# Pacing the transfers that sum weights, and handing over the activations of the down projection one by one

## The chip, the cores and the metric

The kernel runs on one core of a Trainium2 chip. The metric is the device time of one execution in microseconds (us): here the median of three runs of the kernel before, and later of the runs of the changed kernel beside it.

## The reference, cut to what matters

Two transformer-like blocks run one after the other on a sequence of 1024 tokens with 1024 features, all in float32. What the change touches lies at three places: the modulation vectors at the very start, the up projection, and the down projection.

```python
def modulation(c, w, b, n):
    m = jax.nn.silu(c) @ w + b
    return jnp.split(m, n, axis=-1)

def modulated_norm(x, g, shift, scale):
    return rmsnorm(x, g) * (1.0 + scale[:, None, :]) + shift[:, None, :]

def short_conv_layer(x, c, mod_w, mod_b, norm_g, w_in, conv_w, w_out):
    shift, scale, gate = modulation(c, mod_w, mod_b, 3)
    h = modulated_norm(x, norm_g, shift, scale)
    proj = h @ w_in
...
def _conv_ffn(h, w_up, conv_w, conv_b, w_down):
    u = h @ w_up
    a, g = jnp.split(u, 2, axis=-1)
    s = a.shape[1]
    ap = jnp.pad(a, ((0, 0), (CONV_WIDTH - 1, 0), (0, 0)))
    a = ap[:, 0:s] * conv_w[0] + ap[:, 1:s + 1] * conv_w[1] + ap[:, 2:s + 2] * conv_w[2] + conv_b
    return (jax.nn.gelu(a, approximate=False) * g) @ w_down
```

## The kernel before, in words

Activations are kept transposed, features on the partitions and tokens along the free side, in two halves of 512 tokens. Each float32 product is made of three float32r products: a weight tile (a *piece*, `wr`, 128 x 512 elements, 256 KB) is loaded by SP, its rounded part `wh` is written by ScalarE (a CAST), and the rest `wl` by VectorE (a subtraction). Activations are split in the same way into the two halves of an `act` tile. `proj` (line 432) then runs three matmuls for each 128 x 128 block of weights and 512 tokens. Pieces form one list, `stream`, in the order of use; loads run 5 pieces ahead of the use, the casts 3 and the subtractions 2.

The program is written by Python code that keeps a rough clock for each engine (`Sched`). Side jobs are generators: what each one yields says when it wants its next turn on that clock, and `proj` gives turns between its matmuls. So the numbers in `yield` set where in the order an instruction stands, and nothing else: on the chip an engine runs its queue in that order, and waits only for the semaphores of real dependences.

**The start.** SP loads four tiles of x (`xk`, 512 KB each), then strips of the modulation weights (`mw`, two DMAs of 256 KB a strip) with a piece of `w_in` after most of them. VectorE multiplies each strip by silu(c) and adds it up (`acc`); PE sums over partitions (`sm`); VectorE makes `mod_a` and `gs_a` and from these the normed activations `nt`, which ScalarE and VectorE split into `act`. Only then can the first projection (`pj`) run. Four strips give the first quarter of the features.

**The weight sums.** The up projection is done with sums of blocks of its weights, so that fewer products are needed. `weight_sums` (line 1431) has these sums made by 128 DMAs on POOL's queue, from DRAM to DRAM, 64 rows of 1408 elements each (352 KB), some of which add to what stands at their destination. They are first needed in `up_rest`, some 2000 us into the run. POOL's queue also carries the kernel's stores (`x_d`, `k_d`, `v_d`, `q_d`, ...), each of which waits for the engine that makes its data. A POOL DMA waits for no more than the eighth DMA before it on that queue, and for its data.

**The down projection.** It runs over 22 `act` tiles, eight jobs of 66 matmuls for the first half of the tokens, and then eight jobs for each quarter of the second half. The tiles come from DRAM (`act_d`): `act_side` (line 1614) loads one (`al`) and splits it once there is room. Room is a count: `big` tiles in use may not exceed 34, and `free` lowers the count. A half's 22 tiles are given up together by `drop` when the last job (j == 7) is written; the same `drop` serves the other three projections that use `res_jobs` (line 765).

Of the kernel before, what the change touches and what calls it, by code (L numbers as in the profile page):

```python
# [9 lines left out]
F32 = mybir.dt.float32  # L10
# [8 lines left out]
HT = 512  # L19
NJ = 8  # L20
DFF = 2816
NF = DFF // 128
# [26 lines left out]
N_G = 7  # L49
M_BR = 4  # L50
M_WO = 5
T_SUM = 110.0
E_SUM = 9.0
R_SUM = 64


class Sched:
# [204 lines left out]
def tile_body(  # L262
# [14 lines left out]
    sch = Sched()  # L277
# [4 lines left out]
    act = sca.activation  # L282

    const = ctx.enter_context(tc.tile_pool(name="const", bufs=1))
# [9 lines left out]
    out = out[0]  # L294
# [10 lines left out]
    def free(n=1):  # L305

        in_use[0] -= n

    def room(n, hold=0):

        while in_use[0] + n > N4:
            yield 0.4
        in_use[0] += hold
# [5 lines left out]
    def sml(w=HT, dt=F32, name="s"):  # L319
        return s2.tile([128, w], dt, nm(name))  # L320
# [7 lines left out]
    def f32(ap):  # L328
        return ap.bitcast(F32)
# [24 lines left out]
    stream = []  # L354
# [44 lines left out]
    A = {}  # L399

    def split_to(key, src, sh=None):

        yield from room(1 + (kept[0] if key[0] in ("h2", "act0") else 0))
        t = big([2, HT], F32R, "act")
        hi, lo = t[:, 0, :], t[:, 1, :]
        if sh is None:
            sca.copy(out=hi, in_=src)
            if src.space == bass.MemoryType.PSUM:
                sch.keep(src)
            yield t  # L410
            vec.tensor_tensor(out=lo, in0=src, in1=f32(hi), op=ALU.subtract)
        else:
            act(out=hi, in_=src, func=ACTF.Identity, bias=sh)
            yield t
            vec.scalar_tensor_tensor(out=lo, in0=src, scalar=sh, in1=f32(hi), op0=ALU.add, op1=ALU.subtract)
        A[key] = t

    def drop(name, half=None):
        for k in [k for k in A if k[0] == name and (half is None or k[2] == half)]:
            del A[k]  # L420
            free()
# [7 lines left out]

        return half if isinstance(half, tuple) else (half, 0, HT)  # L430

    def proj(pieces, name, half):

        h, c0, w = span(half)
        c = slice(c0, c0 + w)
        sch.turn(sch.bank_time())
        ps = bank("pj")[:, 0:w]
        nk = sum(p.nk for p in pieces)
        k = 0
        for pc in pieces:  # L440
            use(pc)
            for i in range(pc.nk):
                a = act_of((name, k, h))
                sch.turn(sch.when((a, pc.h, pc.l)))
                mm(ps, lhsT=pc.h[:, i, :], rhs=a[:, 0, c], start=k == 0, stop=False)
                mm(ps, lhsT=pc.h[:, i, :], rhs=a[:, 1, c], start=False, stop=False)
                mm(ps, lhsT=pc.l[:, i, :], rhs=a[:, 0, c], start=False, stop=k == nk - 1)
                k += 1
        return ps

# [239 lines left out]
    def hs(half):  # L690
        h, c0, w = span(half)
        return slice(h * HT + c0, h * HT + c0 + w)
# [65 lines left out]
    def res_jobs(w, name, gate, x_dram, out_dram, done=None, extra_g=None, ks=((0, 4), (4, 4)), squares=True, pairs=False):  # L758
        st = {}

        def post(j, half, ps, xo):
            n = span(half)[2]
            if pairs:
                if j % 2 == 0:
                    st["pair", half] = big([2, HT], name="xn")
                xn = st["pair", half][:, j % 2, :]
            else:
                xn = sml(n, name="xn")
            vec.scalar_tensor_tensor(out=xn, in0=ps, scalar=V[gate][:, j:j + 1], in1=xo,
                                     op0=ALU.mult, op1=ALU.add)  # L770
            if out_dram is not None:
                store(out_dram[j, :, hs(half)], xn)
            if done is None:
                return
            s = st.setdefault(half, {"x": [], "acc": [None, None]})
            s["x"].append(xn)
            if squares:
                for a, g in enumerate([None, extra_g]):
                    if a and g is None:
                        continue  # L780
                    yield xn
                    sq = sml(name="sq")
                    act(out=sq, in_=xn, func=ACTF.Square, scale=V[g][:, j:j + 1] if g else 1.0)
                    yield sq
                    if j == 0:
                        s["acc"][a] = sq
                    else:
                        vec.tensor_tensor(out=s["acc"][a], in0=s["acc"][a], in1=sq, op=ALU.add)
                if j == 7:
                    yield s["acc"][0]  # L790
                    yield from done(half, st.pop(half))
            elif j in TURNS:
                yield xn
                yield from done(half, s, j)

        def job(j):
            def fn(half, pieces):
                h, c0, n = span(half)
                xo = sml(n, name="xo")
                syn.dma_start(out=xo, in_=x_dram[j, :, hs(half)])  # L800
                ps = proj(pieces, name, half)
                if j == 7 and c0 + n == HT:
                    drop(name, h)
                then(post(j, half, ps, xo))
            return [Piece(w, k, n, j * 128, 128) for k, n in ks], fn
        return [job(j) for j in range(NJ)]
# [104 lines left out]
    def wait(name):  # L911
        while name not in flags:
            yield 0.5
# [517 lines left out]
    def weight_sums():  # L1431

        def W(k, f, n):
            return w_up[512 * k:512 * k + 512, n * DFF + f * HF:n * DFF + (f + 1) * HF]

        while sch.t < T_SUM:
            yield 2.0
        for n in range(2):
            g = [sg_d[i][n] for i in range(4)]
            for to, of, op in ((0, W(0, 1, n), None), (2, W(0, 0, n), None), (0, W(1, 1, n), ALU.add),  # L1440
                               (2, W(0, 1, n), ALU.add), (1, W(0, 0, n), None), (3, W(1, 0, n), None),
                               (1, g[0], ALU.add), (3, g[1], ALU.add)):
                for r in range(0, 512, R_SUM):
                    kw = {"accum_op": op, "max_dma_last_dim": HF * 4} if op else {}
                    pol.dma_start(out=g[to][r:r + R_SUM], in_=of[r:r + R_SUM], **kw)
                    yield E_SUM

# [166 lines left out]
    def act_side(half):  # L1614

        fs = [f + i for f, n in DOWN for i in range(n)]
        for k, f in enumerate(fs):
            yield from wait(("act", f, half))
            yield from room(1)
            sch.spawn(act_one(k, f, half))  # L1620
            yield 0.7

    def act_one(k, f, half):
        t = sml(name="al")
        syn.dma_start(out=t, in_=act_d[f, :, hs(half)])
        yield t
        yield from split_to(("act", k, half), t)

    fin = {}

# [402 lines left out]
```

## Time and profile before

| | |
|---|---|
| median of 3 runs | 2667.33 us (2665.23 to 2668.66) |
| the profiled execution, its own time | 2669.03 us |
| its span, first to last instruction | 2666.9 us |
| mean granted TensorE clock | 0.992 of full |
| PE busy | 2570.2 us (96%) |
| VectorE, ScalarE, POOL busy | 1724.5, 1232.9, 276.0 us |
| DMA queue of SP (q1), of POOL (q0), of ScalarE (q10), share of 16 engines | 48.6%, 16.2%, 0.4% |

PE is the engine that is nearly always busy, so the time is PE's work, the stretches in which PE stands idle, and the stretches in which it runs at the lower of its two clock levels (2.4 and 1.2 GHz). The spans of an execution and its time differ by some 2 us, which lie around the first and last instruction.

### The profile page before, as it was taken

What the parts mean: (1) busy time and instruction counts of PE and PEld (TensorE: products, weight loads), DVE (VectorE), ACT (ScalarE), POOL (GpSimd) and SP (SyncE); (2) the same over time, 40 slices, a digit from 0 to 9 for tenths busy, and PEclk for the clock granted to TensorE, in tenths of its full rate; (3) what the DMA queues carried; (4) which work ended last, traced back from release to release, by engine and by line L of the source; (5) the groups of instructions that cost most, each with busy time, mean ns of one, the idle gap of its engine ahead of it and who ended that gap; (6) DMA issues with size and microseconds to landing.
All of it is one profiled execution on the core that took longest, in us unless ns stands there. A gap on an engine that the chain in (4) does not pass through costs nothing.

```text
span 2666.9 us, 39606 instructions
## 1 busy us (share of the span) xinstructions
PE 2570.2 (96%) x14015; PEld 2126.0 (80%) x14015; DVE 1724.5 (65%) x3137; ACT 1232.9 (46%) x2492; POOL 276.0 (10%) x469
## 2 busy tenths in 40 slices
PE   2999999999999989999999999999999999999898
PEld 1888888889977767778787887888787788888798
DVE  2876666776366687988765556674657766663454
ACT  2521112353155566777674353564536534443343
POOL 3000000122221111211210110000001000000000
PEclk9999999999999999999999999999999999999999
DMA  9865556778798876666885757555454546454575
GB/s 288 279 190 159 160 170 213 247 240 266 210 252 229 250 194 160 185 200 171 224 222 149 223 159 225 167 158 167 155 164 151 173 138 186 141 170 153 165 212 156
DMA packets 536078, 514.64 MB, mean 193 GB/s; under 512 B 30078, under 2 KB 429704, under 8 KB 535880
## 3 DMA queue, kind: packets, MB, share of 16 engines
q1 hardware_dynamic: 497252, 377.01, 48.6%
q0 software_dynamic: 36272, 130.88, 16.2%
q10 hardware_dynamic: 2356, 4.21, 0.4%
q8 instruction: 111, 1.82, 0.3%
q14 instruction: 87, 0.71, 0.1%
HBM read 422.07 MB, written 136.05 MB: 209 GB/s over the span
## 4 chain that ended last, share of the span: by engine, by line
PE 89%; DVE 5%; DMA 2%; SPq 2%; ACT 2%; issue 1%; DVEq 0%; ACTq 0%
PE pj L246 71%; PE pv L246 5%; PE o L246 4%; PE z L246 4%; PE tr L247 3%; SPq L247 2%; DVE om L247 2%; DVE be L247 1%; DVE wl L247 1%; PE sm L247 1%; DVE act L247 0%; DMA wr<-in_w_in_dram 0%; DMA wr<-in_b_w_out_dram 0%; DMA wr<-in_b_w_qz_dram 0%; DMA wr<-in_a_w_in_dram 0%
## 5 line engine op out<-in xcount | busy, mean ns | idle before, releaser
L246 PE MATMUL pj<-act,wh 128*128 128x512 f32 (+1 forms) x6064 | 1837.5, 386 | 21.1 <-ACT act L247 11.6
L246 PEld LDWEIGHTS pj<-act,wh 128*128 128x128 f32 x6064 | 1099.0, 189 | 239.2 <-ACT act L247 13.1
L246 PE MATMUL pj<-act,wl 128*128 128x512 f32 (+1 forms) x3032 | 1158.6, 382 | 1.4 <-DVE wl L247 1.4
L246 PEld LDWEIGHTS pj<-act,wl 128*128 128x128 f32 x3032 | 572.5, 189 | 122.3 <-DVE wl L247 2.7
L247 DVE TENSOR_TENSOR wl<-wr,wh 128x512 fp32r<-128x512 f32 (+1 forms) x752 | 493.5, 676 | 145.4 <-ACT wh L247 144.1
L247 ACT CAST wh<-wr 128x512 fp32r<-128x512 f32 (+1 forms) x752 | 444.3, 615 | 197.6 <-PE pj L246 81.7
L247 ACT COPY aT<-tr 128x512 f32<-128x512 f32 (+3 forms) x272 | 128.6, 504 | 153.4 <-PE tr L247 149.4
L246 PE MATMUL z<-kd,qs 128*128 128x512 f32 (+2 forms) x704 | 166.3, 352 | 0.0
L247 DVE SCALAR_TENSOR_TENSOR acc<-mw,silu_c,acc 128x512 f32<-128x512 f32 x196 | 146.5, 748 | 30.3 <-DMA mw<-in_a_mod_w_dram 27.0
L246 PE MATMUL pv<-wh,act 128*128 128x256 f32 x768 | 141.0, 282 | 0.0
L247 DVE SCALAR_TENSOR_TENSOR xn<-pj,mod,xo 128x512 f32<-128x512 f32 (+1 forms) x40 | 25.7, 643 | 158.6 <-PE pj L246 158.6
L246 PEld LDWEIGHTS z<-kd,qs 128*128 128x128 f32 x704 | 115.1, 192 | 15.5 <-issue 5.3
L247 DVE TENSOR_TENSOR_SCAN om<-om 128x640 f32<-128x640 f32 (+3 forms) x64 | 120.6, 1884 | 7.6 <-ACT om L247 7.6
L246 PEld LDWEIGHTS pv<-wh,act 128*128 128x128 f32 x768 | 119.3, 188 | 0.1
L246 PEld LDWEIGHTS o<-aT,vp 128*64 128x64 f32 (+1 forms) x1440 | 99.6, 150 | 21.7 <-issue 13.0
L246 PE MATMUL o<-aT,vp 128*64 128x128 f32 (+1 forms) x1440 | 116.1, 281 | 0.7 <-ACT aT L247 0.7
L246 PE MATMUL pv<-wl,act 128*128 128x256 f32 x384 | 107.9, 281 | 0.0
L247 POOL DMA_DIRECT2D x_d<-xn x48 | 26.4, 550 | 653.8 <-DVE xn L247 653.6
L247 ACT ACTIVATE p<-p,t 128x256 f32<-128x256 f32 (+7 forms) x128 | 81.2, 636 | 25.0 <-DVE t L247 24.9
L247 ACT ACTIVATE sq<-xn 128x512 f32<-128x512 f32 x48 | 30.5, 636 | 110.2 <-DVE xn L247 105.1
L247 DVE TENSOR_REDUCE t<-sm 128x4 f32<-128x512 f32 x40 | 27.6, 690 | 81.1 <-PE sm L247 81.1
L247 ACT COPY u<-pj 128x512 f32<-128x512 f32 x38 | 22.3, 587 | 124.4 <-PE pj L246 71.1
(225 smaller groups left out, 2450.7 us busy)
## 6 DMA issues: line engine op xcount, KB each, us to landing
wr<-in_w_in_dram SPq DMA_DIRECT2D x136, 256.0 KB, 3.8
mw<-in_w_ada_dram SPq DMA_DIRECT2D x96, 256.0 KB, 3.7
wr<-in_w_down_dram SPq DMA_DIRECT2D x96, 256.0 KB, 3.1
wr<-in_a_w_in_dram SPq DMA_DIRECT2D x80, 256.0 KB, 6.1
wr<-in_w_up_dram SPq DMA_DIRECT2D x66, 256.0 KB, 3.2
wr<-in_b_w_qz_dram SPq DMA_DIRECT2D x64, 256.0 KB, 5.7
qs<-q_d SPq DMA_DIRECT2D x64, 256.0 KB, 9.0
mw<-in_a_mod_w_dram SPq DMA_DIRECT2D x48, 256.0 KB, 6.2
```

The source lines that it names most:

```text
L246: return f(out, *value, **kw)
L247: return f(out=out, **kw)
```

## The change

Three edits. A POOL instruction, a copy of one column of the `wl` piece that was split last at that place of the program, now stands ahead of each of the 128 summing DMAs, so that POOL reaches the DMA only when VectorE has made that piece; the numbers that place the sums are changed, and on the program's clock none is placed between 600 and 880. `proj` gets a flag with which the last job gives up each `act` tile when its three matmuls are written, in place of the `drop` at the end. And `act_side` loads tiles 5 ahead without asking for room, and asks for it only when it splits one.

```diff
-T_SUM = 110.0
-E_SUM = 9.0
+T_SUM = 130.0
+E_SUM = 6.0
+BUSY_SUM = (600.0, 880.0)
 R_SUM = 64
+AHEAD_ACT = 5
...
-    def proj(pieces, name, half):
+    def proj(pieces, name, half, last=False):
...
                 mm(ps, lhsT=pc.l[:, i, :], rhs=a[:, 0, c], start=False, stop=k == nk - 1)
+                if last:
+                    del A[name, k, h]
+                    free()
                 k += 1
...
-                ps = proj(pieces, name, half)
-                if j == 7 and c0 + n == HT:
-                    drop(name, h)
+                ps = proj(pieces, name, half, j == 7 and c0 + n == HT)
...
+        paced = const.tile([128, 1], F32, name="paced")
         while sch.t < T_SUM:
             yield 2.0
...
                     kw = {"accum_op": op, "max_dma_last_dim": HF * 4} if op else {}
+                    while BUSY_SUM[0] < sch.t < BUSY_SUM[1]:
+                        yield 2.0
+                    pol.tensor_copy(out=paced, in_=f32(stream[done_to["l"] - 1].l[:, 0, 0:1]))
                     pol.dma_start(out=g[to][r:r + R_SUM], in_=of[r:r + R_SUM], **kw)
                     yield E_SUM
...
         fs = [f + i for f, n in DOWN for i in range(n)]
-        for k, f in enumerate(fs):
-            yield from wait(("act", f, half))
-            yield from room(1)
-            sch.spawn(act_one(k, f, half))
-            yield 0.7
-
-    def act_one(k, f, half):
-        t = sml(name="al")
-        syn.dma_start(out=t, in_=act_d[f, :, hs(half)])
-        yield t
-        yield from split_to(("act", k, half), t)
+        got = {}
+        for k in range(NF + AHEAD_ACT):
+            if k < NF:
+                yield from wait(("act", fs[k], half))
+                got[k] = sml(name="al")
+                syn.dma_start(out=got[k], in_=act_d[fs[k], :, hs(half)])
+            if k >= AHEAD_ACT:
+                t = got.pop(k - AHEAD_ACT)
+                yield t
+                yield from room(1)
+                sch.spawn(split_to(("act", k - AHEAD_ACT, half), t))
+            yield 0.6
```

The change moves instructions on all engines, since the clock on which the program is written comes out otherwise. SP's queue is the same row for row up to its 101st DMA, which covers the whole start. The first place is POOL's queue at the start, before (`sg_d0a` and the like are the summing DMAs):

```order
L247 DMA rows_293<-in_final_norm_g_dram 8x128
L247 DMA sg_d0a<-in_w_up_dram 64x1408 x8
L247 DMA sg_d2a<-in_w_up_dram 64x1408 x8
L247 DMA sg_d0a<-in_w_up_dram 64x1408 x8
L247 DMA sg_d2a<-in_w_up_dram 64x1408 x5
L247 DMA x_d<-xn_3606 128x512
```

and the same place of the changed kernel:

```order
L249 DMA rows_293<-in_final_norm_g_dram 8x128
L249 COPY paced<-wl_1439 128x1
L249 DMA sg_d0a<-in_w_up_dram 64x1408
L249 COPY paced<-wl_1439 128x1
L249 DMA sg_d0a<-in_w_up_dram 64x1408
L249 COPY paced<-wl_1522 128x1
L249 DMA sg_d0a<-in_w_up_dram 64x1408
```

Before, 29 sums stood with nothing to wait for ahead of the first store; now each waits for a `wl` that is made after the start, and 39 of them stand ahead of that store. POOL's queue as a whole has these sums, before and now: up to the first store of x 29 and 39; from there to the last store of v 27 and 35; from there to the last store of q 21 and none; from there to the end of the first half of `b_w_out` 13 and 9; from there to the first store of a gate 28 and 40; and behind it 10 and 5. The place where they pause, in the changed kernel:

```order
L249 DMA v_d<-vt_5969 128x2x256
L249 COPY paced<-wl_5936 128x1
L249 DMA sg_d2g<-in_w_up_dram 64x1408
L249 DMA v_d<-vt_6037 128x2x256
L249 COPY paced<-wl_5936 128x1
L249 DMA sg_d2g<-in_w_up_dram 64x1408
L249 DMA v_d<-vt_6097 128x2x256
L249 DMA v_d<-vt_6155 128x2x256
L249 DMA v_d<-vt_6238 128x2x256
```

Before, a sum went on standing after every second or third store there.

The last place is ScalarE's queue where the down projection goes from the first half of the tokens to the second. Before (`wh` are weight pieces, `act` the tiles of the second half, `fj` squares of the finished output, first of the seventh and here of the eighth job):

```order
L247 CAST act_24268<-al_24266 128x512
L247 CAST wh_24276<-wr_24211 128x512
L247 ACTIVATE fj_24285,t_23751<-yt_24130 128x128
L247 ACTIVATE fj_24288,t_23751<-yt_24136 128x128
L247 ACTIVATE fj_24291,t_23751<-yt_24142 128x128
L247 ACTIVATE fj_24294,t_23751<-yt_24148 128x128
L247 CAST act_24301<-al_24299 128x512
L247 CAST wh_24314<-wr_24226 128x512
L247 CAST act_24320<-al_24318 128x512
L247 CAST act_24327<-al_24325 128x512
L247 ACT_TABLE_LOAD
```

and in the changed kernel, where these `fj` are those of the seventh job, and the eighth's (`fj_24482` and on) follow 20 rows later:

```order
L249 CAST act_24275<-al_23962 128x512
L249 ACTIVATE fj_24288,t_23868<-yt_24284 128x384
L249 CAST act_24290<-al_23970 128x512
L249 ACTIVATE fj_24296,t_23868<-yt_24292 128x384
L249 ACTIVATE fj_24304,t_23868<-yt_24300 128x384
L249 ACTIVATE fj_24310,t_23868<-yt_24306 128x384
L249 CAST wh_24317<-wr_24223 128x512
L249 CAST act_24321<-al_23985 128x512
L249 CAST act_24329<-al_23992 128x512
L249 CAST act_24336<-al_24000 128x512
L249 CAST act_24343<-al_24273 128x512
```

In both kernels 15 of the 22 tiles of the second half are split around this turn. Before, 2 stood ahead of the eighth job's `fj` and 13 behind; now all 15 stand ahead, among the pieces of the eighth job, and the loads of the first six stand more than ten pieces earlier on SP's queue.

## Rows read from the trace of the kernel before

**Rows 1.** Windows: stretch, its length, busy by engine; clock, DMA share, GB/s.
```profile
0.00:62.00 62.00, 11.62 (x47) 9.35 (x47) 13.19 (x30) 13.71 (x24) 22.31 (x42) 1.00 1.00 285
...
150.00:450.00 300.00, 300.00 (x1332) 243.52 (x1331) 199.32 (x339) 54.56 (x98) 1.63 (x2) 1.00 0.54 168
450.00:680.00 230.00, 229.99 (x1248) 197.29 (x1248) 160.95 (x255) 95.95 (x163) 46.59 (x80) 1.00 0.83 259
680.00:905.00 225.00, 224.62 (x1428) 179.31 (x1425) 131.89 (x217) 110.19 (x261) 40.15 (x66) 1.00 0.82 222
905.00:955.00 50.00, 42.64 (x262) 33.61 (x259) 33.28 (x39) 27.45 (x62) 8.57 (x16) 0.92 0.98 279
955.00:1250.00 295.00, 285.49 (x2114) 232.87 (x2113) 252.67 (x296) 215.63 (x473) 42.41 (x65) 0.99 0.65 180
```

**Rows 2.** Timeline of PE: start, us, instruction, [idle before <- what ended it].
```profile
26.60 1.12 PE L247 MATMUL rb<-ident,t 128*128 128x128 f32 x4 [15.28 <-DVE t L247]
...
48.80 1.87 PE L246 MATMUL sm<-ones,acc 128*128 128x1 f32 x8 [20.23 <-DVE acc L247]
...
61.88 0.79 PE L246 MATMUL pj<-act,wh 128*128 128x512 f32 x1 [7.70 <-ACT act L247]
...
64.76 0.80 PE L246 MATMUL pj<-act,wh 128*128 128x512 f32 x1 [2.08 <-DVE act L247]
```

**Rows 3.** DMA queues of 0 to 62 us: packets, MB, share of 16 engines.
```profile
q0 software_dynamic: 2512, 10.50, 64.2%
q1 hardware_dynamic: 6677, 7.14, 35.5%
```

**Rows 4.** The same of 24 to 36 us.
```profile
q0 software_dynamic: 567, 2.56, 86.1%
q1 hardware_dynamic: 569, 0.55, 17.2%
```

**Rows 5.** The same of 62 to 80 us.
```profile
q1 hardware_dynamic: 8259, 6.06, 112.2%
```

**Rows 6.** Timeline of POOL: the first sums, the last early one, the next store.
```profile
5.15 1.53 POOL L247 DMA_DIRECT2D sg_d0a<-in_w_up_dram  x3
...
40.62 0.78 POOL L247 DMA_DIRECT2D sg_d2a<-in_w_up_dram  x1 [1.14 <-DMA sg_d0a<-in_w_up_dram]
...
447.48 0.82 POOL L247 DMA_DIRECT2D x_d<-xn  x1 [406.07 <-DVE xn L247]
```

**Rows 7.** Timeline at the start: PE at the last x tile, VectorE ahead of the projection.
```profile
9.14 2.18 PE L247 MATMUL xt<-ident,xk 128*128 128x128 f32 x9 [0.84 <-DMA xk<-in_x_dram]
...
61.85 1.53 DVE L247 SCALAR_TENSOR_TENSOR acc<-mw,silu_c,acc 128x512 f32<-128x512 f32 x2
```

**Rows 8.** Windows at the turn of the halves of the down projection.
```profile
2502.03:2516.85 14.82, 14.82 (x73) 12.28 (x72) 3.79 (x7) 5.95 (x15) 0.00 (x0) 1.00 0.51 143
2516.85:2535.99 19.14, 11.51 (x55) 9.10 (x54) 16.91 (x36) 13.68 (x31) 4.60 (x8) 0.68 0.98 333
```

**Rows 9.** The chain that ended last: start, us, what; at and after the turn.
```profile
2516.89 4.91 DMA al<-act_d
...
2563.47 23.42 PE pj L246 x198
```

**Rows 10.** Timeline of SP and PE at the turn.
```profile
2519.68 5.10 SPq L247 DMA_DIRECT2D al<-act_d  x6
...
2517.13 0.60 PE L247 MATMUL yt<-ident,xn 128*128 128x128 f32 x4
```

**Rows 11.** Waits of 905 to 955 us: who for whom, total, times, longest.
```profile
PE tr L247 <- DVE be L247: 7.3, 3, 3.4
...
ACT wh L247 <- DMA wr<-in_b_w_out_dram: 5.7, 2, 3.5
```

**Rows 12.** DMA issues of 905 to 955 us: count, KB, median us to landing.
```profile
sg_d2g<-in_w_up_dram POOLq DMA_DIRECT2D x5, 352.0 KB, 8.8
```

**Rows 13.** Timeline of POOL: its smallest computing instruction on a tile.
```profile
2.08 0.32 POOL masks.py:199 TENSOR_SCALAR_AFFINE_SELECT ident<-ident 128x128 f32<-128x128 f32 x1
```

## The prediction

> **What bounds the kernel now.** I read the windows first. From 150 to 450 us and from 450 to 680 us PE is busy for every microsecond at full clock [rows 1]: nothing that other engines or transfers do there is worth time as long as PE stays fed. What can be won lies where PE is idle or at its lower clock. Three places hold nearly all of it. The first is the start: in the first 62 us PE works 11.62 us [rows 1], and its timeline shows the first `pj` at 61.88 us and the next at 64.76, after waits of 15.28, 20.23, 7.70 and 2.08 us for VectorE and ScalarE [rows 2]; from 64.76 us on it is fed. The second is the stick-breaking attention from 905 to 1250 us, where PE is idle for 7.4 and 9.5 us and the clock means are 0.92 and 0.99 [rows 1]. The third is the turn from the first half of the tokens to the second in the down projection: 11.51 us busy in 19.14 us, at a clock of 0.68 [rows 8].
>
> What sets the start is seen in the queues. In 0 to 62 us the 16 DMA engines are full: 64.2% of their time goes to POOL's queue and 35.5% to SP's [rows 3]. POOL's are the sums: the first is issued at 5.15 us, the 29th at 40.62, and then POOL waits 406 us for the first store [rows 6]. In the middle of this the two queues move almost the same number of packets, 567 and 569, but the sums' packets take 86.1% of the time [rows 4]: a large packet goes for each small one. So the loads of x, `mw` and `wr`, which the first projection needs, crawl. Once the sums are over, SP's queue moves 6.06 MB in the 18 us from 62 to 80 us [rows 5], 0.337 MB a us.
>
> **The change, part by part.**
>
> *The sums leave the start.* No pacing copy can run before VectorE has made a `wl`, and the first `wl` that is named comes well after the first projection, so SP has the DMA engines for itself. Two ways give the time of the second `pj`. By engine time: the sums took 0.642 x 62 = 39.8 us of all 16 engines, and 64.76 - 39.8 = 25.0 us. By bytes: the first four tiles of x are there at 9.14 us, much as now; the last gate ahead of that `pj` is the `acc` that starts at 61.85 us [rows 7], on the seventh strip, with 14 `mw` and two `wr` ahead of it, 16 x 0.262 = 4.19 MB; at 0.337 MB a us that is 12.4 us, so 21.6 us, and 64.76 - 61.85 = 2.9 us more give 24.5. I take 26.5, 2 us later: with the bytes landing so evenly, PE starts with less loaded ahead than it has now. The gain is 64.76 - 26.5 = 38 us. The bounds: 41 us if it starts at 24, and 25 if the engines' work in this stretch, 11.62 + 13.19 + 13.71 us [rows 1], ran wholly in a row, 38.5 us, behind the first 1.2 us. After that the shift stays: the program that follows is PE's work.
>
> *Where the sums go.* One costs 39.8 / 29 = 1.37 us of all engines. Up to the first store 39 now run beside PE, between 100 and 445 us: 53 us of engine time in 345, so the share rises from 0.54 to about 0.70. Each may hold SP's queue up for its own 1.4 us, and pieces are loaded five ahead; a piece is 12 matmuls long here, so this lead hides it: nothing. To the end of v there are 8 more, 11 us in some 250, from 0.83 to about 0.87. PE runs there without a gap beside 27 sums now [rows 1]; I take 1 us lost, between 0 and 5. From there to 905 us 21 sums are gone, 29 us of engine time, from 0.82 to about 0.7. From 905 to 955 us the DMA share is 0.98 [rows 1], ScalarE stands 5.7 us for pieces of `b_w_out`, blocks its queue with the attention's sigmoids behind it, and PE then waits 7.3 us for `be` [rows 11]; five sums and more are in flight there, each landing after 8.8 us [rows 12]. PE's loss there is 50 - 42.64 = 7.4 us, and a mean clock of 0.92 with two levels means 16% of 50 us at half rate, 4 us: 11.4 in all. With the pause ahead of it I take half back, 6 us, of 0 to 11. From the end of this half of `b_w_out` to the gates there are 12 more, 16 us in 300, from 0.65 to 0.71; PE already loses 9.5 us there and the program stands in another order: 1 us lost, between 5 gained and 8 lost.
>
> *The copies.* There are 128. None was in the trace; the nearest row is POOL's 0.32 us for a whole tile of 128 columns [rows 13], so I bound one by nothing and by that. What stands behind one on POOL is its sum and the next store; a store in the program stands behind work that is later than the `wl` named, so its data is seldom there first. The copy also keeps its `wl` tile from being overwritten until POOL has read it; with POOL busy for 276 us of the run, it is there in time. I take 1 us for all, of 0 to 5. The Trainium skill, SBUF - State Buffer, section Who interferes with whom, speaks against them: a VectorE instruction with two SBUF inputs and a GpSimd instruction that reads SBUF block each other for the whole instruction. No run here shows it yet; by it each copy could hold up a subtraction or be held up by one, which is a rival below.
>
> *The turn of the halves.* Seven tiles of the second half are split early, then room is out until the last job's `drop`. So 13 casts, their loads (six issued at 2519.68 us in a queue of 5.10 us [rows 10]; one wait of 4.91 us stands in the chain [rows 9]) and their subtractions all come while PE stands. The 55 PE instructions of that window are 51 matmuls at 23.42 / 198 = 0.118 us [rows 9] and 4 transposes at 0.15 us [rows 10]: 6.0 + 0.6 = 6.6 us. The rest, 19.14 - 6.6 = 12.5 us, is the loss, idle time and lower clock together [rows 8]. Now a tile comes free every three matmuls of the eighth job, which lasts some 15 us, its loads are out already, and 15 casts at about 0.5 us stand among six pieces' casts, where ScalarE works 5.95 of 14.82 us now [rows 8]. The last is needed only 14 tiles into the next job. I take 11.5 us gained; the bounds are 12.5, and 5 if only the wait for the loads goes. The same flag in the other three projections moves splits of tiles that PE isn't short of: nothing.
>
> **The sum**: -38 - 6 + 1 + 1 + 1 - 11.5 = -52.5 us. Against the profiled execution's own time of 2669.0 us that is 2616.5; the median shown is 1.7 us lower, so I forecast **2615 us**.
>
> **The rivals.** (1) The start is held by something else once the DMA engines are free: by the chain of `acc`, `sm`, `nt` and `act` on three engines, or by pieces. VectorE is idle for 49 of 62 us, which speaks against it. At worst 25 us are gained there, so about 2628; chance 0.12. (2) The sums cost PE where they now run: the stretch to 680 us turns short of transfers, or the attention behind the pause does, with 40 sums for 28. PE's full windows beside sums speak against it, the gaps of 905 to 955 us for it. With 8 to 25 us lost it gives 2625 to 2640; chance 0.10. (3) Slower: while a sum is in flight, SP's packets alternate with its own, and VectorE, in order, stands for a late `mw` with a `wl` behind it; if each of the 74 sums ahead of the pause cost PE over 52.5 / 74 = 0.71 us, half of the 1.37 us it takes, the gain would be eaten, and at the full 1.37 us it would be 2615 + 101 = 2716. The rows from 450 to 680 us, with sums and no gap, speak against it: 0.02. (4) The turn stays blocked, since splits on ScalarE wait for PE's releases ahead of pieces' casts: 2615 + 11.5 = 2626; chance 0.05. (5) Copies and subtractions hold each other up: 128 x 0.32 = 41 us at most on VectorE, which is idle for a third of the run; only the 40 or so copies in the attention, where VectorE is busy for 252.67 of 295 us [rows 1], can reach PE, 13 us, 2628. It is the page's rule above that would do this; chance 0.02. That the sums would run early anyway is excluded by the waits on `wl`.
>
> **How the numbers follow.** My forecast has 0.69. Its own range is 2602 to 2626: 41 and 12.5 us with 10 in the middle on one side, 34 and 9 with 2 lost in the middle on the other (2667.3 - 41 - 12.5 - 10 = 2604, 2667.3 - 34 - 9 + 2 = 2626), and 2 us for the runs' own spread. Rivals 1, 2, 4 and 5 reach 2640. So the range is 2600 to 2640. Differences within 0.2%, 5.3 us, are about what a measurement can't tell from none; all cases but the third lie far below that, so faster 0.96, same 0.02, slower 0.02.
>
> **What would show it.** Right: in the first 62 us POOL issues no sum, SP's queue has nearly all of the DMA time, and the second `pj` starts at 24 to 30 us; PE full from there; sums one by one between 100 and 450 us at a DMA share near 0.70 with PE at full clock; a shorter wait of ScalarE for `b_w_out`; no idle PE at the turn, and the chain there made of PE. Wrong: a first `pj` after 35 us, new waits of PE for `wl` or of VectorE for `mw` between 100 and 700 us, or more idle time in the attention than its 17 us.

## The result, and the profile after

The changed kernel takes **2624.14 us** (median of 4 runs, 2622.03 to 2627.16) where the kernel before, run beside it, takes 2667.89: a ratio of 0.9839, 95% interval 0.9822 to 0.9856, so 43.75 us or 1.6% faster. The forecast was 2615, its range 2600 to 2640. The profiled execution took 2622.03 us, 47.0 less than that of before.

The windows of the changed kernel, with the columns of [rows 1]; the whole program has moved up by 39 us, so 866 to 916 us here is 905 to 955 us there:

```profile
0.00:62.00 62.00, 46.28 (x209) 37.29 (x210) 48.61 (x94) 34.29 (x61) 4.17 (x13) 0.97 0.91 285
150.00:450.00 300.00, 300.00 (x1326) 243.26 (x1326) 191.16 (x322) 58.32 (x104) 48.81 (x96) 1.00 0.77 226
450.00:640.00 190.00, 189.66 (x1066) 164.38 (x1066) 130.86 (x209) 82.41 (x140) 56.94 (x103) 1.00 0.88 258
866.00:916.00 50.00, 43.16 (x274) 33.61 (x273) 37.76 (x49) 30.60 (x70) 4.32 (x8) 0.97 0.81 247
916.00:1211.00 295.00, 284.91 (x2038) 232.46 (x2040) 235.62 (x285) 204.96 (x442) 73.44 (x112) 0.99 0.68 188
2469.00:2484.00 15.00, 15.00 (x74) 12.43 (x73) 12.28 (x21) 11.56 (x26) 0.00 (x0) 1.00 0.82 253
2484.00:2500.00 16.00, 16.00 (x138) 16.00 (x138) 13.32 (x31) 10.08 (x24) 4.33 (x8) 1.00 0.85 262
```

The first and the last two lines are the gain: PE works 46.28 of the first 62 us in place of 11.62, and there is no idle time where the halves turn. Between them the picture of before seems to be there still: 43.16 busy of 50 us at `b_w_out` (42.64 before), 284.91 of 295 in the attention (285.49 before). But a window of fixed length tells how busy PE is, and not how far the program has come in it: the attention's window holds 2038 PE instructions where it held 2114.

PE's timeline at the first projection, and the DMA queues of 0 to 62 us, beside [rows 2] and [rows 3]:

```profile
24.48 0.80 PE L248 MATMUL pj<-act,wh 128*128 128x512 f32 x1 [0.35 <-ACT act L249]
28.03 0.50 PE L248 MATMUL pj<-act,wh 128*128 128x512 f32 x1 [2.75 <-DVE act L249]
```
```profile
q1 hardware_dynamic: 19904, 17.57, 89.8%
q0 software_dynamic: 192, 0.05, 0.4%
```

POOL's queue has 0.05 MB in this stretch where it had 10.50, SP's 17.57 MB where it had 7.14, and the second `pj` starts at 28.03 us, not 64.76.

To see where time is won and lost along the run, I take the same VectorE instructions in every trace as marks. They write `xn` at the end of a `res_jobs` projection, or in the norm behind one. In the changed kernel's timeline of VectorE five of them are

```profile
407.19 0.74 DVE L249 SCALAR_TENSOR_TENSOR xn<-pj,mod_a,xo 128x512 f32<-128x512 f32 x1
...
934.29 0.74 DVE L249 SCALAR_TENSOR_TENSOR xn<-pj,mod_b,xo 128x512 f32<-128x512 f32 x1
...
1450.08 0.74 DVE L249 SCALAR_TENSOR_TENSOR xn<-xn,veca,rb 128x512 f32<-128x512 f32 x1
...
2482.63 0.75 DVE L249 SCALAR_TENSOR_TENSOR xn<-pj,mod,xo 128x512 f32<-128x512 f32 x1 [1.48 <-PE pj L248]
...
2491.41 0.48 DVE L249 SCALAR_TENSOR_TENSOR xn<-pj,mod,xo 128x256 f32<-128x256 f32 x1
```

They are P1 (first of `a_w_out`), P2 (first of `b_w_out`, first half), P3 (last of the norm behind its second half, and so behind most of the attention), P4 (last of the down projection's first half) and P5 (first of its second half). P6 is the last one of all, at 2611.13. In the kernel before they stand at 446.43, 973.96, 1484.1, 2515.56, 2537.46 and 2657.82. So the changed kernel is ahead by 39.2 us at P1, 39.7 at P2, **34.0** at P3, 32.9 at P4, 46.1 at P5 and 46.7 at P6. The start gives 39, the turn gives 13, and between P2 and P3 almost 6 us are lost where the forecast has 1. The marks are read from one execution of each kernel. Among kernels with the same instructions in the same order a stretch of some 500 us differs by 3 to 5 us from trace to trace, so smaller differences of marks mean little; the times of the kernels, medians of several executions, are the firmer evidence.

### The profile page after: what moved, and what is told of

Same layout as the page of the kernel before. It is cut to its first block, busy times and chain, and to the rows that moved or that the text cites. A ratio compares the mean times of both kernels' runs of the same rounds, so it can differ in the third digit from the quotient of the medians.

```text
span 2620.2 us, 39902 instructions
## 1 busy us (share of the span) xinstructions
PE 2563.2 (98%) x14015; PEld 2118.3 (81%) x14015; DVE 1724.2 (66%) x3137; ACT 1238.8 (47%) x2498; POOL 333.0 (13%) x598
## 4 chain that ended last, share of the span: by engine, by line
PE 87%; DVE 6%; issue 3%; DMA 2%; ACT 1%; SPq 0%; POOL 0%; DVEq 0%; ACTq 0%; POOLq 0%
PE pj L248 70%; PE z L248 4%; PE o L248 4%; PE pv L248 4%; PE tr L249 3%; DVE om L249 2%; DVE wl L249 1%; DVE be L249 1%; PE sm L249 1%; DVE act L249 1%; DMA wr<-in_b_w_qz_dram 1%; DVE t L249 0%; DMA wr<-in_b_w_out_dram 0%; DVE p L249 0%; SPq L249 0%
## 5 line engine op out<-in xcount | busy, mean ns | idle before, releaser
L248 PE MATMUL z<-kd,qs 128*128 128x256 f32 (+2 forms) x704 | 164.3, 351 | 0.1
L249 POOL COPY paced<-wl 128x1 f32<-128x1 f32 x128 | 67.2, 525 | 512.0 <-DVE wl L249 490.0
L248 PEld LDWEIGHTS o<-aT,vp 128*64 128x64 f32 (+1 forms) x1440 | 97.5, 147 | 23.4 <-issue 12.6
L249 ACT ACTIVATE om<-z 128x384 f32<-128x384 f32 (+2 forms) x128 | 68.9, 539 | 22.3 <-PE z L248 22.0
L249 PE MATMUL tr<-ident,be 128*128 128x128 f32 x416 | 61.0, 281 | 18.2 <-DVE be L249 16.9
```

Of the source, the lines that this page charges most:

```text
L248: return f(out, *value, **kw)
L249: return f(out=out, **kw)
```

## The experiments

That each of the three edits has its own gain is called theory A in what follows. For the loss of 6 us there were two to begin with. **M1:** the sums' traffic, which now stands in the attention behind the pause, costs PE time. **M2:** it is not the sums, but something else in the middle: copies, another order of the instructions, or an earlier start that meets loads which take their own time. After the first four runs a third was split off from M2, **theory O, order**: the edits make the Python planner write the attention in another order, and that order is worse, whatever sums and copies do.

### One part alone, and the sums without their traffic

`pace_only` adds to the kernel before

```diff
+        paced = const.tile([128, 1], F32, name="paced")
...
+                    pol.tensor_copy(out=paced, in_=f32(stream[done_to["l"] - 1].l[:, 0, 0:1]))
```

> The kernel before with nothing but the copies ahead of the sums: no pause, the old spacing of the sums, the old turn of the halves. If the start's gain is the sums leaving it (theory A), the first store of x is made 39 us earlier than in the kernel before, and 29 sums run by then beside PE for nothing. Whether these 39 us are then kept tells where the middle loses: if the 4 to 5 us that the changed kernel loses between 930 and 1450 us come from sums that now stand in the attention behind the pause (theory M1), nothing is lost here, since no pause moves them, and the time is 2667.9 - 39 = 2629. If they come from the work being shifted against loads that take their own time, or from the copies (theory M2), they are lost here too: 2633 to 2634.

`turn_only` is the changed kernel without the copies and the pause, with the sums' old numbers:

```diff
-T_SUM = 130.0
-E_SUM = 6.0
-BUSY_SUM = (600.0, 880.0)
+T_SUM = 110.0
+E_SUM = 9.0
...
-                    while BUSY_SUM[0] < sch.t < BUSY_SUM[1]:
-                        yield 2.0
-                    pol.tensor_copy(out=paced, in_=f32(stream[done_to["l"] - 1].l[:, 0, 0:1]))
```

> The kernel before with only the new act_side and the release of tiles one by one; the sums stand as before, without copies or pause. If the turn's gain is its own (theory A), the two traces are alike up to the down projection within a microsecond, the gap between the halves closes by 12.5 to 13.5 us and the time is 2667.9 - 13 = 2655. If part of the 13 us that the changed kernel gains there comes from the sums or from another order earlier in the program (rival), less is gained here: 2658 to 2662 with a gap of several microseconds left at the turn. If releases on PE hold up ScalarE's casts of pieces (rival 4 of the prediction), 2667.

`before_small` and `after_small` cut the sum's DMA to 16 columns; they leave out the summed weights, and the up projection reads plain blocks of the weights instead:

```diff
-                    pol.dma_start(out=g[to][r:r + R_SUM], in_=of[r:r + R_SUM], **kw)
+                    sch.note("pool", "dma_start", g[to][r:r + R_SUM], [of[r:r + R_SUM]])
+                    nc.gpsimd.dma_start(out=g[to][r:r + R_SUM, 0:16], in_=of[r:r + R_SUM, 0:16], **kw)
...
-        return Piece(sg_d[n - 1]["ag".index(which)], 0, 4, m * 128, 128)
+        return Piece(w_up, 0, 4, "ag".index(which) * DFF + m * 128, 128)
```

> The kernel before, with every sum's DMA cut to 16 of its 1408 columns (4 KB in place of 352), at the same places in every queue; the summed weights are left out, and the up projection reads plain blocks of the weights in their place. So PE's, VectorE's and ScalarE's work is the same and only the sums' traffic is gone. If the burst at the start costs what the share of DMA time says (theory A), 38 to 41 us are gained by the first store of x. If the pause was worth 6 us at the first half of b_w_out, as the prediction has it, another 5 to 7 us are gained between 890 and 1050 us, and the time is about 2623; if SP's own loads fill the DMA engines there without any sum (theory M2), nothing is gained there: 2628 to 2629.

> The changed kernel, with every sum's DMA cut to 16 of its 1408 columns, copies and order kept; the summed weights are left out, and the up projection reads plain blocks of the weights in their place. What it gains on the changed kernel is all that the sums' traffic still costs there. If sums in the attention behind the pause cost PE time (theory M1), 4 to 6 us come back between 920 and 1450 us: 2618 to 2620. If the loss in the middle comes from the order of the instructions and from SP's own loads (theory M2), the time stays within 1.5 us of the changed kernel's 2624.

Measured, against 2667.27 us:

| | us | ratio, 95% interval | ahead of before at P1, P2, P3, P4, P5 (us) |
|---|---|---|---|
| `pace_only` | 2643.45 | 0.9910 (0.9895 to 0.9925) | 37.8, 41.5, 24.2, 23.5, 25.2 |
| `turn_only` | 2672.96 | 1.0022 (1.0013 to 1.0031) | 2.0, 0.5, -16.8, -18.2, -5.0 |
| `before_small` | 2625.24 | 0.9839 (0.9822 to 0.9855) | 36.9, 39.8, 40.7, 40.4, 42.2 |
| `after_small` | 2625.36 | 0.9843 (0.9829 to 0.9858) | 37.7, 35.6, 28.3, 27.1, 40.2 |

The start and the turn do what was said, 37 to 38 and 13 us, but two of the four times were missed by far. `pace_only` is at 2643, 9 us beyond both of its theories, since it loses 17 us between P2 and P3. `turn_only`, which was to gain 13 us, is slower than the kernel before: it loses 17 us in the same stretch, and the turn gives back only 13. And `after_small`, in which the sums move hardly anything, is as slow there as the changed kernel: it falls from 35.6 to 28.3 us ahead. That refutes theory M1. `before_small`, with an earlier start and no such loss, takes the earlier start out of M2. What the three bad ones have in common, and `before_small` has not, is that their instructions stand in another order than in the kernel before.

`before_small` speaks on the pause too. The windows of 865 to 915 us in it, and the one wait of PE there:

```profile
865.00:915.00 50.00, 42.82 (x270) 33.15 (x268) 35.14 (x43) 28.84 (x66) 9.08 (x16) 0.99 0.84 240
```
```profile
PE tr L247 <- DVE be L247: 7.2, 5, 2.0
```

Nearly without traffic of sums PE still waits 7.2 us for `be` (7.3 in [rows 11]) and is busy for 42.82 us (42.64 in [rows 1]). ScalarE stands for pieces of `b_w_out` for 0.4 us in all where it stood 5.7, and PE waits just the same. Only the clock, 0.99 for 0.92, is better, and some 3 us are gained by P2 (36.9 us ahead at P1, 39.8 at P2), which puts the time, 2625, between the two expected. These 3 us can't be put down to the missing traffic: `release_only` (below), with the same order up to there and all of its sums, gains 2.9 between the same marks.

### The order kept

If order is the cause, the same edits must be free of it when the planner doesn't notice them. `turn_down` is `turn_only` with the release one by one in the down projection alone:

```diff
-                ps = proj(pieces, name, half, j == 7 and c0 + n == HT)
+                ps = proj(pieces, name, half, name == "act" and j == 7 and c0 + n == HT)
+                if name != "act" and j == 7 and c0 + n == HT:
+                    drop(name, h)
```

> The kernel before with the new act_side, and the release of tiles one by one in the down projection alone; in the other three projections the old drop stays. The instructions on PE are those of the kernel before, row for row, up to some 2000 us. If turn_only was slower only because the release in the other projections changes the order in which the attention is written (theory O, order), the two traces are alike to the down projection, the turn gives back 13 us, and the time is 2667.3 - 13 = 2654. If the new act_side itself is what costs (rival), the loss of 17 us ahead of 1500 us has no reason to be gone: 2667 to 2673.

`pace_silent` issues the copies past the planner's clock:

```diff
-                    pol.tensor_copy(out=paced, in_=f32(stream[done_to["l"] - 1].l[:, 0, 0:1]))
+                    nc.gpsimd.tensor_copy(out=paced, in_=f32(stream[done_to["l"] - 1].l[:, 0, 0:1]))
```

> The kernel pace_only again, with the same copies at the same places, except that the program's clock doesn't count them: every other instruction then stands in the order of the kernel before on each engine. If the 16 us that pace_only lost in the attention between 1040 and 1390 us come from another order there (theory O), they are gone, the start's 37 to 39 us are kept, and the time is 2627 to 2630. If they come from the copies themselves, by holding up VectorE, or POOL's stores, or the wl tiles (theory C, and rival 5 of the prediction), they stay: 2643.

> turn_down and pace_silent together: copies that the clock doesn't count, the old spacing of the sums and no pause, the new act_side, and the release one by one in the down projection alone. If the two gains are independent and the order is what spoils them (theory O): 2667.3 - 39 - 13 = 2615, about 9 us faster than the changed kernel. If the attention loses time whenever the start is earlier (rival: a work shifted against its transfers), 2620 or more.

`placed` has a second generator that issues copies and sums at the changed kernel's places, without telling the clock, while the old one only tells it:

```diff
-                    nc.gpsimd.tensor_copy(out=paced, in_=f32(stream[done_to["l"] - 1].l[:, 0, 0:1]))
-                    pol.dma_start(out=g[to][r:r + R_SUM], in_=of[r:r + R_SUM], **kw)
+                    sch.note("pool", "dma_start", g[to][r:r + R_SUM], [of[r:r + R_SUM]])
                     yield E_SUM
...
+    def placed_sums():
...
+                    while 600.0 < sch.t < 880.0:
+                        yield 2.0
+                    nc.gpsimd.tensor_copy(out=paced, in_=f32(stream[done_to["l"] - 1].l[:, 0, 0:1]))
+                    nc.gpsimd.dma_start(out=g[to][r:r + R_SUM], in_=of[r:r + R_SUM], **kw)
+                    yield 6.0
```

> silent_both with the sums at the places of the changed kernel: from 130 on, 6 apart, none between 600 and 880 on the program's clock, while that clock goes on counting them where the kernel before has them, so that the order of all other instructions stays that of silent_both. The pause and the places are then all that differs. If the pause is worth what the prediction says, 6 us between 890 and 1050 less 2 us in the stretches that get more sums, 2611; if SP's own loads fill the DMA engines there without sums (theory M2), and the sums behind the pause cost nothing either, 2614 to 2616; if they do cost PE in the attention (theory M1), 2619.

Measured, against 2666.78 us:

| | us | ratio, 95% interval | ahead of before at P1, P2, P3, P4, P5 (us) |
|---|---|---|---|
| `turn_down` | 2654.41 | 0.9951 (0.9936 to 0.9966) | 0.3, 1.5, 3.9, 3.0, 16.1 |
| `pace_silent` | 2628.57 | 0.9850 (0.9832 to 0.9868) | 39.6, 37.1, 39.2, 38.9, 40.7 |
| `silent_both` | 2613.17 | 0.9798 (0.9782 to 0.9813) | 40.1, 39.4, 42.6, 42.1, 55.2 |
| `placed` | 2614.45 | 0.9796 (0.9781 to 0.9811) | 37.2, 39.8, 40.7, 39.8, 52.9 |

Theory O had 2654, 2627 to 2630, 2615, and for a pause worth nothing 2614 to 2616: all four came, within 2 us. The copies themselves cost nothing (15 us between `pace_only` and `pace_silent`, which differ only in order); the release in the other three projections cost `turn_only` 18.5 us; and `silent_both`, at 2613.17 us for 2624.14, is 11 us faster than the changed kernel. `placed`, with the pause and the changed kernel's places, is no faster than `silent_both`.

From P2 to P3, in windows with the columns of [rows 1], here `turn_only`, `turn_down`, the changed kernel and `placed`:

```profile
973.40:1500.90 527.50, 502.79 (x3231) 411.14 (x3230) 395.38 (x719) 345.45 (x758) 76.09 (x119) 0.98 0.69 186
```
```profile
972.50:1480.20 507.70, 495.85 (x3230) 405.80 (x3229) 395.38 (x719) 342.44 (x756) 75.93 (x119) 1.00 0.71 193
```
```profile
934.30:1450.10 515.80, 499.98 (x3230) 406.33 (x3229) 394.72 (x719) 349.88 (x762) 111.49 (x182) 0.99 0.72 196
```
```profile
934.10:1443.40 509.30, 496.75 (x3230) 406.16 (x3229) 395.13 (x719) 342.27 (x756) 118.26 (x182) 1.00 0.73 199
```

The work is the same: 3230 PE instructions (one more in the first), VectorE's 395 us. What differs is idle time, 24.7 us in `turn_only` for 11.9 in `turn_down`, and PE's busy time, 502.8 for 495.9, at a mean granted clock of 0.98 for 1.00. Between the changed kernel and `placed` it is the same on a smaller scale: 15.8 us idle for 12.6, and 500.0 busy for 496.8, at 0.99 for 1.00.

`pace_only` shows one such gap well. Its timelines, in order ScalarE, VectorE and PE:

```profile
1182.37 1.28 ACT L247 ACT_TABLE_LOAD   x1
1183.67 0.60 ACT L247 ACTIVATE om<-z 128x512 f32<-128x512 f32 x1
1184.16 0.59 ACT L247 ACTIVATE be<-z 128x512 f32<-128x512 f32 x1
1184.77 1.28 ACT L247 ACT_TABLE_LOAD   x1
...
1187.27 1.28 ACT L247 ACT_TABLE_LOAD   x1
...
1191.26 2.24 ACT L247 CAST wh<-wr 128x512 fp32r<-128x512 f32 x4
```
```profile
1191.99 1.29 DVE L247 TENSOR_TENSOR wl<-wr,wh 128x512 fp32r<-128x512 f32 x2 [14.55 <-ACT wh L247]
```
```profile
1192.01 0.58 PE L246 MATMUL pv<-wh,act 128*128 128x256 f32 x1 [6.62 <-ACT wh L247]
```

The order puts sigmoids (`om`, `be`) between exponentials (`p`), so ScalarE changes its function table three times in 5 us, and the cast of the next pieces stands behind all that. VectorE stands 14.55 us for it, PE 6.62. Behind the gap PE is at its lower clock level for a while: the granted clock is 0.50 from 1187 to 1195 us, and 1.00 again from 1196 on. The planner doesn't know which order is good on the chip: its clock only approximates. The changed kernel has 48 table loads, as `pace_only` has, and the kernel before 42; but `turn_only` has 44 and loses as much, and `after_downflag` (below) loses 13 us with 40, so table loads are one form of this and not the cause as such.

### The copies, the two halves of the turn, and one more order

`copies3_silent` has the silent copy three times. `fetch_only` and `release_only` each take one half of the turn out of `silent_both`. `fetch_only` gives the tiles up together again:

```diff
-                ps = proj(pieces, name, half, name == "act" and j == 7 and c0 + n == HT)
-                if name != "act" and j == 7 and c0 + n == HT:
+                ps = proj(pieces, name, half, False)
+                if j == 7 and c0 + n == HT:
                     drop(name, h)
```

`release_only` keeps that release and puts the old `act_side` and `act_one` back. `after_downflag` puts `turn_down`'s edit of `proj`'s call into the changed kernel.

> silent_both with three copies ahead of each sum in place of one, 256 more, none counted by the program's clock, so that all other instructions keep their order. If a copy costs PE nothing (the prediction's bounds of 0 to 0.32 us each, with nobody behind it that PE waits for), 2613, within 3 us. If copies and VectorE's subtractions hold each other up (rival 5), about 80 more stand in the attention, where VectorE is busy for 85% of the time; at the 0.18 us that the shortest copy of the changed kernel takes that is 14 us, 2627, and at the mean of 0.53 us 42 us, 2655, with longer subtractions in the trace.

> silent_both with only half of what the turn has: act_side loads five tiles ahead without room, but the 22 tiles of the first half are given up together behind the eighth job, as before. All else keeps its order. The prediction's lower bound for the turn was 5 us, if only the wait for the loads goes. If the loads were half of the loss at the turn, 5 to 7 of the 13 us stay: 2613 + 7 = 2620. If the 13 casts and subtractions are what PE waits for, 0 to 3 stay: 2624 to 2626. If the loads were all of it: 2613.

> silent_both with the other half of what the turn has: tiles are given up one by one in the eighth job, but each is loaded only once there is room, as before. If room is what the loads and casts wait for, they now run during the eighth job's 15 us and nearly all of the 13 us stay: 2613 to 2615. If a load that is issued so late lands too late (4.9 us were waited for one before), PE waits at the first tiles of the second half: 2618 to 2621.

> The changed kernel with the release one by one in the down projection alone; the other three projections give their tiles up together, as before. If that release is what makes the order in the middle bad (turn_only against turn_down speaks for it, 20 us), the 6 to 8 us that the changed kernel loses between 930 and 1450 us come back: 2617. If the copies that the clock counts do it too (pace_only against pace_silent, 15 us), the middle comes out at some other price, since this is yet another order: 2624 to 2640.

Measured, against 2669.41 us:

| | us | ratio, 95% interval | ahead of before at P1, P2, P3, P4, P5 (us) |
|---|---|---|---|
| `copies3_silent` | 2612.06 | 0.9788 (0.9773 to 0.9802) | 39.7, 41.5, 44.8, 42.9, 56.0 |
| `fetch_only` | 2624.23 | 0.9831 (0.9817 to 0.9846) | 40.1, 40.9, 43.6, 42.8, 46.1 |
| `release_only` | 2612.86 | 0.9792 (0.9775 to 0.9808) | 38.4, 41.3, 44.8, 43.5, 56.1 |
| `after_downflag` | 2633.36 | 0.9867 (0.9853 to 0.9882) | 38.9, 37.3, 23.6, 23.0, 36.1 |

The 256 further copies cost nothing. The turn's gain is the release alone: without it 3.3 us are gained from P4 to P5, of which 1.3 are gone again by the end, and without the early loads 12.6 of 13.1 are there, and the time is that of `silent_both`. What PE waits for in `fetch_only`, in its timeline, are the splits:

```profile
2477.81 0.38 PE L247 MATMUL pj<-act,wh 128*128 128x256 f32 x1 [0.86 <-DVE act L248]
2480.22 0.39 PE L247 MATMUL pj<-act,wh 128*128 128x256 f32 x1 [0.59 <-DVE act L248]
2482.88 0.39 PE L247 MATMUL pj<-act,wh 128*128 128x256 f32 x1 [2.01 <-DVE act L248]
2485.74 0.58 PE L247 MATMUL pj<-act,wh 128*128 128x256 f32 x1 [1.03 <-DVE act L248]
```

`after_downflag` missed 2617 and lies in the 2624 to 2640 of its other case. It is slower than the changed kernel by 9 us, 8 of them lost between P2 and P3. So the release in the other projections isn't bad as such: it costs 18.5 us on top of the kernel before and gains 9 on top of the counted copies and the pause. Each edit draws another order, and what the order costs doesn't add up over edits.

All traces side by side, from P2 to P3: nine kernels in the planner's old order for this stretch (before, `before_small`, `turn_down`, `pace_silent`, `silent_both`, `placed`, `copies3_silent`, `fetch_only`, `release_only`) take 506.6 to 510.1 us, whatever their sums and copies do. In their traces the instructions of PE, ScalarE and VectorE stand in this stretch in the same order, row for row. The five in other orders (four orders, since `after_small` has the changed kernel's) take 515.8 (changed kernel), 517.4 (`after_small`), 523.8 (`after_downflag`), 527.4 (`pace_only`, with 48 PE instructions more in the stretch) and 527.5 (`turn_only`). The planner also chooses each tile's buffer by its clock, so "order" here stands for both the places of the instructions and the buffers; no run tells these two apart.

## Why the prediction was right, and where it was not

The range held and the two large terms were right in cause and nearly in size; the middle was 9 us worse than forecast.

- **The sums leave the start: 38 forecast, 39.2 measured** (P1; 37 to 40 in every kernel whose sums leave the start or shrink). The second `pj` came at 28.03 us, 1.5 later than taken, which alone would be 36.7. Nearly all of the rest is that PE's first matmuls are long for less of the time: in its timeline one of `pj` with `wl` takes 0.63 us up to 72.2 us before and up to 30.7 us now, and 0.40 soon after. The same matmul right behind these long ones starts 38.9 us earlier than before.
- **The sums beside PE up to the end of v, and the copies: 2 us lost forecast, none measured.** From P1 to P2 the changed kernel keeps its lead. PE is busy for 300.00 of 300 us at a DMA share of 0.77 where 0.70 was forecast.
- **The relief at `b_w_out`: 6 us forecast, none found.** The granted clock of the window rose from 0.92 to 0.97, but PE's lead is 39.2 us at P1 and 39.7 at P2. This step failed. It joined full DMA engines, ScalarE's wait for `b_w_out` and PE's wait for `be` to one chain because they stood in one window. In the changed kernel's waits of 866 to 916 us the first link is gone and the last is not:

```profile
PE tr L249 <- DVE be L249: 6.8, 4, 2.6
...
ACT wh L249 <- DMA wr<-in_b_w_out_dram: 0.7, 1, 0.7
```

  `before_small` shows the same without any sum, and `placed` is 1.3 us slower than `silent_both` by the medians, which is no difference. The five kernels with silent copies and the old order up to there need 514.0 to 519.3 us from the last `xn` of `a_w_out` to the last of `b_w_out`'s first half, and `placed` 514.2, so a gain of some 2 us may be hidden in this scatter.
- **Behind the pause: 1 us lost forecast for the sums and another order; 5.7 measured** from P2 to P3. The bounds, 5 gained to 8 lost, held it. The prediction gave two causes, 12 more sums and another order, and worked out only the sums; the runs show the order alone, since `after_small` loses as much without the sums' traffic and `placed` nothing with it. And "the same flag in the other three projections: nothing" is a step that failed outright: it looked at which tiles PE is short of, and not at what the count of tiles does to the planner. Added to the kernel before it costs 18.5 us, and in the changed kernel, whose order is another anyway, it gains 9.
- **The turn: 11.5 forecast, 13.1 measured** (P4 to P5), above the upper bound of 12.5. It is the release, as the prediction had it; the lower bound of 5 us, for the loads alone, was too high.

By the marks the parts are 39.2, 0.5, -5.7, -1.1, 13.1 and 0.6 us, together 46.6 of the 47.0 between the two profiled executions. The forecast's own range, 2602 to 2626, has the 2 us of spread between runs at its lower end only; 2624 lies inside it either way, near the upper end. Of the rivals none came true by its mechanism. Rival 2 named the right place and, with 2625 to 2640, nearly the time, but for a wrong reason. Rival 3, slower by the traffic, is refuted by 74 sums ahead of the pause with no loss. Rival 4: no idle time at the turn. Rival 5: the mean subtraction takes 676 ns in the kernel before, without any copy, 676 in `silent_both`, and 677 with three copies a sum. The first and the last of these:

```profile
L247 DVE TENSOR_TENSOR wl<-wr,wh 128x512 fp32r<-128x512 f32 (+1 forms) x752 | 493.5, 676 | 145.4 <-ACT wh L247 144.1
...
L248 DVE TENSOR_TENSOR wl<-wr,wh 128x512 fp32r<-128x512 f32 (+1 forms) x752 | 495.0, 677 | 149.7 <-ACT wh L248 140.4 <-issue 5.8 <-PE pj L247 1.9
```

So VectorE's subtractions aren't held up by the copies. What stays open is which rows of the order cost the changed kernel its 6 to 7 us. PE's waits from P2 to P3 come to some 15 us there and to 12 in `placed`. Most of the difference is in the waits for `be`, of which none is over 2 us; they are, first in the changed kernel and then in `placed` (total, times, longest),

```profile
PE tr L249 <- DVE be L249: 10.1, 14, 1.7
...
PE tr L248 <- DVE be L248: 7.3, 11, 1.1
```

They were not taken apart further.

## What to carry to other kernels

Where a planner writes the program, an edit that is free on the chip may still change the order everywhere behind it: cost the order as a term of its own, with the spread that it has shown (here 6 to 21 us in one stretch of some 510), and measure an edit with the order held fixed before you judge it. Transfers that nobody needs soon must not stand where a start waits for its loads, even on another queue. Where a set of tiles is given up together at the end of a pass, look at what waits for the last of them: giving them up one by one was worth more here than loading ahead.

## What the runs showed of the hardware

A copy of one column on POOL has a median of 426 ns in the changed kernel but takes up to 2050, 525 on average, above the 320 that bounded it:

```profile
L249 POOL COPY paced<-wl x128: 183/426/2050, 143.0 to 1318.1; 128x1 f32<-128x1 f32 x128
```

The twelve longest, of 1.24 us and more, stand beside VectorE's scans. In the timelines of POOL and VectorE one is

```profile
1005.03 2.05 POOL L249 COPY paced<-wl 128x1 f32<-128x1 f32 x1 [3.10 <-DVE wl L249]
```
```profile
1004.81 2.29 DVE L249 TENSOR_TENSOR_SCAN om<-om 128x1024 f32<-128x1024 f32 x1
```

The copy starts 0.22 us after the scan and ends with it, at 1007.1 us. The Trainium skill, SBUF — State Buffer, section Who interferes with whom, says that a VectorE instruction with two SBUF inputs contends with a GpSimd (POOL) instruction that reads SBUF, for a port pair that one of them holds alone, and that the order of issue decides which of them blocks. The scan is given `om` as both of its inputs, and on POOL's side the trace agrees: the copy comes second and lasts until the scan ends. The other side, a VectorE instruction held up by a copy of 0.18 us, isn't shown by any run here: the means above don't move.
